# Turning the MLPs' inner activations and the output of seven heads by transposing transfers instead of on TensorE

## The chip, the cores and the metric

The kernel runs on one core of a Trainium2 chip. The metric is the device time of one execution in microseconds (us). The kernel before takes 2459.45 us, the median of three runs (2459.42, 2459.45 and 2463.46 us).

## The reference

A two-layer decoder trunk on one sequence of 256 tokens with 2048 channels, all in float32. Layer 0 is a retention layer with 8 heads, layer 1 a multi-head latent attention with 16 heads; each is followed by an MLP with 8192 inner channels. What matters here:

```python
def retention(...):
    ...
    o = o * lax.rsqrt(jnp.mean(o * o, axis=-1, keepdims=True) + RMS_EPS)   # per head, 512 values
    o = o.reshape(b, s, H * dv).astype(h.dtype)
    return (jax.nn.silu(gate) * o) @ w_out

def sq_relu_mlp(h, w1, w2):
    return jnp.square(jax.nn.relu(h @ w1)) @ w2
```

Both products need their left operand with the channel that is summed over on the partitions. The products that make that operand (`h @ w1`, a head's output) leave it with the tokens on the partitions. So between the two it has to be turned: 256 tokens x 8192 inner values in each MLP, 256 x 512 in each head.

## The kernel before, in words

**Products.** The 256 tokens are two tiles of 128 (t = 0, 1). Float32 accuracy comes from splitting each operand into a high and a low part (`split`, line 213): ScalarE rounds the high part (line 216), VectorE subtracts it to make the low part (line 217), and TensorE does three matmuls for one product (lines 409 to 411: high by high, high by low, low by high). Weights stream from HBM in quads of 1 MB (`quad`, line 321): one transfer issued by SP (SyncE) into one of three buffers `raw` (line 324), then split into tiles `wh` and `wl` (128 x 1024, five buffers each). A plain quad has eight products of 128x128 by 128x512. A quad "of seven" first forms sums of the weight blocks on VectorE (lines 363, 372 and 373), needs sums of the activations too (`with_sums`), and has seven products. `gemm_pair` (line 386) runs eight such quads and then takes the results out (`pair_out`, line 427): ScalarE copies six accumulators to SBUF (line 432), VectorE adds the rest (lines 434 to 448).

**The order of the work.** A program queue sets it: `tick` counts one per quad, `later(n, fn)` puts fn n ticks ahead, and at each tick the functions that are due write their instructions. Each engine runs its instructions in the order in which they end up in its list, and SP its transfers too.

**The MLPs.** `mlp` (line 864) has four groups in each layer. A group does two pairs of the first weight matrix (called here the even and the odd pair, 8 quads each; `u_` in the names), then two pairs of the second (`d_`). When a pair `u_` is done its result (2 token tiles x 2 blocks of 512 values) goes to `up` (line 871): four Relu on ScalarE (line 877), then `turn(0)` and, a tick later, `turn(1)`. A `turn` takes one block of 512 values of both token tiles and turns it in two halves k2. For each half, `transposed` (line 230) does four 128x128 transposes on TensorE into a PSUM bank (line 235), ScalarE squares the bank into SBUF (line 886), and the result is split (`hid`) and, for odd halves, summed (`hid_sum`, `hid_more`). A block thus has 8 transposes; a group has four blocks, two of the even pair and two of the odd one. The even pair's blocks are turned while the odd pair's quads run, the odd pair's while the first `d_` pair runs; that one needs the odd pair's blocks in its quads 4 to 7.

**The heads.** `ret_out` (line 748) makes a head's output y (two token tiles x 512), and its `turn` (line 767) turns it in the same way, 8 transposes a head, while the next head's quads run (for the last head, those of the output projection).

**Buffers.** The small SBUF tiles of 2 KB a partition all come from one ring of 14 (`f2k`, line 72).

Of the kernel before, what the change touches and what calls it, by code (L numbers as in the profile page):

```python
# [14 lines left out]
I32 = mybir.dt.int32  # L15
AF = mybir.ActivationFunctionType
# [19 lines left out]
P = 128  # L36
NT = 2
S = NT * P
# [28 lines left out]
def yoco(ctx: ExitStack, tc: tile.TileContext, a):  # L67
# [162 lines left out]
    def transposed(srcs, name):  # L230

        tp = bank("tp", [2, S], name)
        for j in range(2):
            for t in range(NT):
                nc.tensor.transpose(tp[:, j, t * P : (t + 1) * P], srcs(t, j), ident)
        return tp

# [510 lines left out]
    def ret_out(h, s, v, gate, y_act):  # L748
# [17 lines left out]

        def turn():
            for k2 in range(2):
                tp = transposed(lambda t, j: ys[t][:, (2 * k2 + j) * P : (2 * k2 + j + 1) * P], f"ytp{h}{k2}")
                yt = act_tile(f"y{h}{k2}")  # L770
                more = None
                if len(y_act) in (HEAD if h < RH // 2 else LATE):
                    u = f2k([2, S], f"yu{h}{k2}")
                    nc.scalar.copy(u, tp)
                    split_act(yt, u)
                    more = with_sums(u, f"y{h}{k2}")
                else:
                    split_act(yt, tp)
                y_act.append((yt, more))
# [84 lines left out]
    def mlp(layer, act, r, done):  # L864
        w1, w2 = a[f"mlp_w1_{layer}"], a[f"mlp_w2_{layer}"]
        f0 = 0
        for gi, nf in enumerate(GROUPS):
            hid, blocks = [], []
            last = gi == len(GROUPS) - 1

            def up(c, p, hid=hid, blocks=blocks):
# [3 lines left out]
                for t in range(NT):  # L875
                    for i in range(2):
                        nc.scalar.activation(c[t][i], c[t][i], AF.Relu, scale=r[t])

                def turn(i):
                    for q in (2 * i, 2 * i + 1):  # L880
                        name = f"hid{layer}_{p}{q}"
                        tp = transposed(
                            lambda t, j: c[t][q // 2][:, (q % 2 * 2 + j) * P : (q % 2 * 2 + j + 1) * P], f"{name}_tp"
                        )
                        u = f2k([2, S], f"{name}_u")
                        nc.scalar.activation(u, tp, AF.Square)
                        v = act_tile(name)
                        split_act(v, u)
                        blocks.append((v, with_sums(u, name) if len(blocks) in ODD else None))
                        hid.append(v)  # L890
# [402 lines left out]
```

## Time and profile before

| | |
|---|---|
| median of the runs | 2459.45 us |
| span of the profiled execution (first to last instruction) | 2456.3 us |
| TensorE matmul (PE) busy | 2446.2 us |
| VectorE (DVE) busy | 2212.2 us |
| ScalarE (ACT) busy | 1641.3 us |
| GpSimd (POOL) busy | 238.0 us |
| bytes moved by DMA | 521.05 MB, 212 GB/s |
| the two MLPs | 721 to 1389 us and 1774 to 2456 us of the span |

The profile lists instructions by engine, source line, operation and tile: `u_c<-u_wh,n` is a matmul that writes the accumulator `u_c` from the weights `u_wh` and the activations `n`. Start and duration are in microseconds, means in nanoseconds. PE is TensorE's matmuls, PEld its weight loads; matmuls overlap in the pipeline, so the time that one costs is the step from its start to the start of the next, not its duration. The profiled execution's own time is not listed apart from its span; the median of the runs lies 3.15 us above the span.

### The profile page before, as it was taken

What the parts mean: (1) busy time and instruction counts of PE and PEld (TensorE: products, weight loads), DVE (VectorE), ACT (ScalarE), POOL (GpSimd) and SP (SyncE); (2) the same over time, 40 slices, a digit from 0 to 9 for tenths busy, and PEclk for the clock granted to TensorE, in tenths of its full rate; (3) what the DMA queues carried; (4) which work ended last, traced back from release to release, by engine and by line L of the source; (5) the groups of instructions that cost most, each with busy time, mean ns of one, the idle gap of its engine ahead of it and who ended that gap; (6) DMA issues with size and microseconds to landing.
All of it is one profiled execution on the core that took longest, in us unless ns stands there. A gap on an engine that the chain in (4) does not pass through costs nothing.

```text
span 2456.3 us, 31721 instructions
## 1 busy us (share of the span) xinstructions
PE 2446.2 (100%) x11614; PEld 2057.6 (84%) x11614; DVE 2212.2 (90%) x2919; ACT 1641.3 (67%) x2307; POOL 238.0 (10%) x287
## 2 busy tenths in 40 slices
PE   9999999999999999999999999999999999999999
PEld 7888888888888888888888888998888888888887
DVE  7899899888899999999999998777899999999998
ACT  6566666556676767667676777577667667676674
POOL 6400001000000010010110001101000100100100
PEclk9999999999999999999999999999999999999999
DMA  8555569556565586695786555444555865957854
GB/s 309 207 201 191 192 202 259 191 183 224 197 218 194 196 254 218 207 272 187 241 253 213 200 202 180 155 162 173 197 199 205 252 228 194 262 198 229 264 209 170
DMA packets 93692, 521.05 MB, mean 212 GB/s; under 512 B 11104, under 2 KB 12512, under 8 KB 40288
## 3 DMA queue, kind: packets, MB, share of 16 engines
q1 hardware_dynamic: 72144, 472.83, 55.2%
q0 software_dynamic: 21248, 46.15, 8.9%
q8 instruction: 91, 1.49, 0.2%
q14 instruction: 65, 0.53, 0.1%
q10 hardware_dynamic: 144, 0.05, 0.0%
HBM read 479.14 MB, written 39.85 MB: 211 GB/s over the span
## 4 chain that ended last, share of the span: by engine, by line
PE 92%; DVE 2%; ACT 1%; issue 0%; DMA 0%; POOL 0%; ACTq 0%; DVEq 0%
PE u_c L411 7%; PE u_c L410 7%; PE u_c L409 7%; PE d_c L411 6%; PE d_c L410 6%; PE d_c L409 6%; PE rp_c L411 3%; PE rp_c L409 3%; PE rp_c L410 3%; PE u_p L411 2%; PE u_p L410 2%; PE u_p L409 2%; PE rq_acc L307 2%; PE rk_acc L307 2%; PE ro_c L411 2%; PE ro_c L409 2%
## 5 line engine op out<-in xcount | busy, mean ns | idle before, releaser
L217 DVE TENSOR_TENSOR d_wl<-d_raw,d_wh 128x1024 fp32r<-128x1024 f32 (+1 forms) x256 | 278.7, 1111 | 31.6 <-ACT d_wh L216 31.6
L217 DVE TENSOR_TENSOR u_wl<-u_raw,u_wh 128x1024 fp32r<-128x1024 f32 (+1 forms) x256 | 279.3, 1113 | 29.8 <-ACT u_wh L216 29.8
L409 PE MATMUL u_c<-u_wh,n 128*128 128x512 f32 x712 | 278.3, 392 | 0.0
L411 PE MATMUL u_c<-u_wh,n 128*128 128x512 f32 x712 | 277.2, 389 | 0.0
L410 PE MATMUL u_c<-u_wl,n 128*128 128x512 f32 x712 | 277.2, 389 | 0.0
L409 PE MATMUL d_c<-d_wh,hid 128*128 128x512 f32 x706 | 275.4, 392 | 0.5 <-ACT d_wh L216 0.5
L411 PE MATMUL d_c<-d_wh,hid 128*128 128x512 f32 x706 | 275.0, 390 | 0.0
L410 PE MATMUL d_c<-d_wl,hid 128*128 128x512 f32 x706 | 274.8, 389 | 0.0
L216 ACT CAST u_wh<-u_raw 128x1024 fp32r<-128x1024 f32 (+1 forms) x256 | 241.3, 973 | 49.6 <-PE u_c L411 24.1
L216 ACT CAST d_wh<-d_raw 128x1024 fp32r<-128x1024 f32 (+1 forms) x256 | 240.3, 971 | 39.9 <-PE d_c L411 16.6
L216 ACT CAST d_wh<-d_u 128x1024 fp32r<-128x1024 f32 x106 | 108.1, 1051 | 119.7 <-DVE d_u L373 82.6
L216 ACT CAST u_wh<-u_u 128x1024 fp32r<-128x1024 f32 x104 | 106.2, 1052 | 116.0 <-DVE u_u L373 77.3
L411 PEld LDWEIGHTS u_c<-u_wh,n 128*128 128x128 f32 x712 | 133.7, 188 | 27.8
L410 PEld LDWEIGHTS u_c<-u_wl,n 128*128 128x128 f32 x712 | 133.8, 188 | 27.4 <-DVE u_wl L217 0.3
L409 PEld LDWEIGHTS u_c<-u_wh,n 128*128 128x128 f32 x712 | 133.7, 188 | 27.0
L409 PEld LDWEIGHTS d_c<-d_wh,hid 128*128 128x128 f32 x706 | 132.6, 188 | 28.2 <-ACT d_wh L216 1.4
L411 PEld LDWEIGHTS d_c<-d_wh,hid 128*128 128x128 f32 x706 | 132.5, 188 | 27.6
L410 PEld LDWEIGHTS d_c<-d_wl,hid 128*128 128x128 f32 x706 | 132.6, 188 | 27.5 <-DVE d_wl L217 0.4
L216 ACT CAST rp_wh<-rp_raw 128x1024 fp32r<-128x1024 f32 x112 | 103.8, 945 | 74.2 <-PE rp_c L411 49.2
L217 DVE TENSOR_TENSOR rp_wl<-rp_raw,rp_wh 128x1024 fp32r<-128x1024 f32 x112 | 119.7, 1090 | 16.4 <-ACT rp_wh L216 16.2
L217 DVE TENSOR_TENSOR u_wl<-u_u,u_wh 128x1024 fp32r<-128x1024 f32 x104 | 123.5, 1222 | 3.1 <-ACT u_wh L216 2.8
L217 DVE TENSOR_TENSOR d_wl<-d_u,d_wh 128x1024 fp32r<-128x1024 f32 x106 | 125.8, 1221 | 0.0
(570 smaller groups left out, 6505.3 us busy)
## 6 DMA issues: line engine op xcount, KB each, us to landing
u_raw<-in_mlp_w SPq DMA_DIRECT2D x128, 1024.0 KB, 5.4
d_raw<-in_mlp_w SPq DMA_DIRECT2D x128, 1024.0 KB, 4.9
rp_raw<-in_ret_w_gv SPq DMA_DIRECT2D x56, 1024.0 KB, 4.8
ro_raw<-in_ret_w_out SPq DMA_DIRECT2D x32, 1024.0 KB, 4.9
uq_raw<-in_mla_w_uq SPq DMA_DIRECT2D x24, 768.0 KB, 4.3
rq_raw<-in_ret_w_qk SPq DMA_DIRECT2D x16, 1024.0 KB, 4.9
rk_raw<-in_ret_w_qk SPq DMA_DIRECT2D x16, 1024.0 KB, 4.8
xh<-d_c POOLq DMA_DIRECT2D x48, 256.0 KB, 6.1
```

Source lines behind the costliest of these rows:

```text
L216: nc.scalar.copy(h, src)
L217: return nc.vector.tensor_tensor(l, src, h.bitcast(F32), op=ALU.subtract)
L307: nc.tensor.matmul(acc[f], wh[:, cols], a.rearrange("p i s -> p (i s)"), start=k == 0, stop=k == nk - 1)
L409: nc.tensor.matmul(dst, ah, bh, start=n == 0, stop=False)
L410: nc.tensor.matmul(dst, ah, bl, start=False, stop=False)
L411: nc.tensor.matmul(dst, al, bh, start=False, stop=n == total[key] - 1)
```

## The change

Of the four blocks of a group in each MLP, three are no longer turned on TensorE: both blocks of the even pair and block 1 of the odd pair. Block 0 of the odd pair stays (`turn_on_pe`). Heads 0 to 6 are no longer turned on TensorE either; head 7 stays. That takes 8 transposes from each of 24 blocks and 7 heads.

In their place, a 32-bit value is seen as two 16-bit halves. `turn_by_dma` copies each token tile's 128x512 block on ScalarE into a tile with all low and all high halves apart (`parts`, 128 x 2 x 512 of 16 bits): two copies of 1024 elements a block. Two or three ticks later SP issues four transposing transfers of 128x512 16-bit values, SBUF to SBUF (two token tiles x two halves), into two tiles `turned`. Then, for each k2, `joined` puts the halves together again: two copies of 512 elements on ScalarE into `u`, which is squared in place (MLP) and split as before. The Relu of a block moves from `up` to its `turn`. The outputs of the heads now always go by way of a tile `u` in SBUF; before, some were split straight from PSUM.

```diff
+    def halves_of(v):
+        return v.bitcast(U16).rearrange("p (n two) -> p two n", two=2)
+
+    def turn_by_dma(blocks, name, wait, steps, then):
+
+        parts = [f2k([2, 512], f"{name}_h{t}", U16) for t in range(NT)]
+        for t in range(NT):
+            nc.scalar.copy(parts[t], halves_of(blocks[t]))
+
+        def turn():
+            turned = [f2k([4, S], f"{name}_t{i}", U16) for i in range(2)]
+            for t in range(NT):
+                for i in range(2):
+                    nc.sync.dma_start_transpose(turned[i][:, :, t * P : (t + 1) * P], parts[t][:, i])
+            for k2 in range(2):
+                later(steps[k2], lambda k2=k2: then(turned, k2))
+
+        later(wait, turn)
+
+    def joined(turned, k2, u):
+
+        for i in range(2):
+            dst = halves_of(u.rearrange("p j s -> p (j s)"))[:, i]
+            nc.scalar.copy(dst, turned[i][:, 2 * k2 : 2 * k2 + 2].rearrange("p j s -> p (j s)"))
...
         def turn():
+            if h < RH - 1:
+                turn_by_dma(ys, f"y{h}", 3, (0, 1), join)
+                return
             for k2 in range(2):
                 tp = transposed(lambda t, j: ys[t][:, (2 * k2 + j) * P : (2 * k2 + j + 1) * P], f"ytp{h}{k2}")
...
                 need(r, NT)
                 c = summed(c)
-                for t in range(NT):
-                    for i in range(2):
-                        nc.scalar.activation(c[t][i], c[t][i], AF.Relu, scale=r[t])
-
-                def turn(i):
-                    for q in (2 * i, 2 * i + 1):
...
+                def turn(i):
+                    for t in range(NT):
+                        nc.scalar.activation(c[t][i], c[t][i], AF.Relu, scale=r[t])
+                    if p % 2 and not i:
+                        turn_on_pe()
+                        return
+                    turn_by_dma(
+                        [c[t][i] for t in range(NT)], f"hid{layer}_{p}{i}", 2 if p % 2 else 3, (0, 1),
+                        lambda turned, k2: square(turned, i, k2),
+                    )
+
+                def square(turned, i, k2):
+                    name = f"hid{layer}_{p}{2 * i + k2}"
+                    u = f2k([2, S], f"{name}_u")
+                    joined(turned, k2, u)
+                    nc.scalar.activation(u, u, AF.Square)
+                    split_up(u, name)
```

49 lines of the change are left out of this document (27 added, 22 removed).

## The prediction

> **What bounds the kernel now.** I read the page first (engines, chain), then what TensorE waited for, then the places where it transposes, then each stretch of the MLPs.
>
> ```profile
> span 2456.3 us, 31721 instructions
> PE 2446.2 (100%) x11614; PEld 2057.6 (84%) x11614; DVE 2212.2 (90%) x2919; ACT 1641.3 (67%) x2307; POOL 238.0 (10%) x287
> PE 92%; DVE 2%; ACT 1%; issue 0%; DMA 0%; POOL 0%; ACTq 0%; DVEq 0%
> ```
>
> ```profile
> PE idle L131 <- DVE zeros L128: 1.2, 1, 1.2
> PE rg_acc L279 <- ACT a L218: 0.7, 1, 0.7
> ```
>
> The chain that ends last is 92% TensorE, and these two rows are TensorE's longest waits in the whole run, both in its first microseconds. So TensorE is not merely busy, it is fed: in the MLPs and heads what it no longer has to do comes off the time, as long as the others can feed it that much faster. DVE at 90% is the next limit.
>
> **What is removed.** A block's eight transposes, in the list of PE's matmuls and in the chain:
>
> ```profile
> 770.56 0.40 PE L411 MATMUL u_c<-u_wh,n 128*128 128x512 f32 x1
> 770.79 1.03 PE L235 MATMUL hid_tp<-cst,u_c 128*128 128x128 f32 x8
> 771.58 0.47 PE L409 MATMUL u_c<-u_wh,n 128*128 128x512 f32 x1
> 771.90 0.39 PE L410 MATMUL u_c<-u_wl,n 128*128 128x512 f32 x1
> 772.12 0.39 PE L411 MATMUL u_c<-u_wh,n 128*128 128x512 f32 x1
> 772.35 0.40 PE L409 MATMUL u_c<-u_wh,n 128*128 128x512 f32 x1
> ```
>
> ```profile
> 237.09 0.87 PE ytp L235 x8
> 770.95 0.87 PE hid_tp L235 x8
> ```
>
> From 771.90 to 772.35 are two plain steps, 0.45 us. The two steps from 770.56 to 771.90 take 1.34 with the transposes between them, so these cost 0.89; the chain has 0.87, for a head's block as for an MLP's. I take 0.88. Removed are 24 blocks (3 of 4, 4 groups, 2 layers) and 7 heads, 31 in all: 31 x 0.88 = 27.3 us, all on the path. That is the most that there is to gain.
>
> **What is added, engine by engine.** I look at one group, by pair: odd `u_` pair (the even pair's two blocks are turned in it), first `d_` pair (the odd pair's two blocks), then two pairs without any; last a head.
>
> ```profile
> 765.30:808.60 43.30, 43.30 (x200) 36.03 (x200) 40.96 (x52) 31.62 (x43) 0.00 (x0) 1.00 0.57 195
> 808.60:851.90 43.30, 43.30 (x200) 36.02 (x199) 41.39 (x52) 31.61 (x43) 0.00 (x0) 1.00 0.56 195
> 851.90:892.70 40.80, 40.80 (x181) 33.80 (x180) 37.49 (x41) 25.55 (x31) 6.96 (x8) 1.00 0.89 257
> 892.70:933.50 40.80, 40.80 (x181) 33.80 (x180) 37.06 (x41) 25.47 (x31) 6.90 (x8) 1.00 0.90 257
> 160.00:228.00 68.00, 68.00 (x336) 57.31 (x335) 62.59 (x96) 41.89 (x56) 2.44 (x6) 1.00 0.55 189
> ```
>
> (Columns: length, busy time of PE, PEld, DVE, ACT, POOL, then the clock and the DMA share.)
>
> ScalarE, per block: two copies of 1024 elements and four of 512. The trace has no copy of 16-bit halves; the nearest rows are 32-bit ones of the same counts.
>
> ```profile
> 767.13 2.97 ACT L216 CAST u_wh<-u_raw 128x1024 fp32r<-128x1024 f32 x3
> 769.97 2.22 ACT L877 ACTIVATE u_c<-u_c,n_r 128x512 f32<-128x512 f32 x3
> 806.93 1.08 ACT L432 COPY u_c<-u_c 128x512 f32<-128x512 f32 x2
> 807.88 1.10 ACT L432 COPY u_p<-u_p 128x512 f32<-128x512 f32 x2
> ```
>
> Three casts of 1024 take 2.84 us from start to start, 0.95 each; two copies of 512 take 0.95, 0.475 each. A block adds 2 x 0.95 + 4 x 0.475 = 3.8 us; squares and splits stay as many as they were. Over 31 blocks that is 118 us on an engine with 815 idle; it costs nothing as long as it is hidden. The cover is thinnest in the odd `u_` pair: two blocks bring ACT from 31.6 to 39.2, while PE falls from 43.3 to 41.5 there. In the first `d_` pair it is 35.4 of 42.4, in a head some 46 of 67. The copies' price from both sides: no saving from below the 32-bit price can shorten anything, since ACT is not the path; twice the price is the third rival.
>
> VectorE does the same work as before, only later. In the odd `u_` pair that is 40.96 us in 41.5. Its 2.3 idle us sit at the pair's end:
>
> ```profile
> 805.63 1.23 DVE L217 TENSOR_TENSOR d_wl<-d_raw,d_wh 128x1024 fp32r<-128x1024 f32 x1 [1.76 <-ACT d_wh L216]
> 785.03 1.23 DVE L217 TENSOR_TENSOR u_wl<-u_u,u_wh 128x1024 fp32r<-128x1024 f32 x1
> 786.87 0.19 PEld L410 LDWEIGHTS u_p<-u_wl,n_more 128*128 128x128 f32 x1
> ```
>
> The first row's wait can shrink without harm. The other two are the thinnest place of the pair: a `wl` ends at 786.26, TensorE loads it at 786.87, 0.6 us ahead. This is where the blocks' splits and sums crowd the start of the pair now; moved three ticks on, they leave that start and fall among quads 4 to 6, so the lead should first grow, then be used up. With DVE at 99% of the pair, a late ScalarE instruction can still make TensorE wait. I allow 0.5 us in each of the eight odd `u_` pairs, 4 us: between nothing and the 1.8 that the pair saves, nearer to nothing as the first `d_` pair, next, has 1.0 to spare and the two after it 3 each.
>
> SP, per block: four transposing transfers of 128 KB, each holding SP and its queue for some time w, and a wait of SP for the copies. Behind them stand the weight loads.
>
> ```profile
> u_raw<-in_mlp_w SPq DMA_DIRECT2D x128, 1024.0 KB, 5.4
> dec<-in_decay SPq DMA_DIRECT2D x8, 128.0 KB, 4.9
> 765.04 0.33 SPq L324 DMA_DIRECT2D u_raw<-in_mlp_w  x1
> 772.58 0.33 SPq L324 DMA_DIRECT2D u_raw<-in_mlp_w  x1
> 776.66 0.33 SPq L324 DMA_DIRECT2D u_raw<-in_mlp_w  x1
> 815.85 0.33 SPq L324 DMA_DIRECT2D d_raw<-in_mlp_w  x1
> L152 POOL DMA_DIRECT2D xh<-d_c x48 | 41.6, 866 | 784.6 <-DVE d_wl L217 439.6 <-ACT d_p L432 229.3 <-DVE u_wl L217 109.2
> q1 hardware_dynamic: 72144, 472.83, 55.2%
> ```
>
> No transposing transfer is in this trace. From below: SP's 0.33 us for an issue; the bytes themselves, at q1's rate (472.83 MB in 55.2% of 2456 us, 349 GB/s), are 0.38. From above: 4.9, the landing of a 128 KB transfer, if each waited for the one before. I take 0.9, near the 0.866 that GpSimd takes to issue one, as a transposing issue is the more laborious.
>
> Does 0.9 stay hidden? The even pair's first four transfers stand behind the load of 765.04 and ahead of that of 772.58 (quad 4). They wait for the copies: the Relus end near 770.7 once two are left for later, then 1.9 of copies, so 772.6. Quad 4's load goes at 772.6 + 4w and lands 5.4 later; the second block's transfers go ahead of quad 5's load, now at 776.66, which goes no earlier than 772.9 + 8w. Where they are needed:
>
> ```profile
> 783.66 1.06 ACT L216 CAST u_wh<-u_raw 128x1024 fp32r<-128x1024 f32 x1 [0.23 <-PE u_c L411]
> 788.23 0.39 PE L409 MATMUL u_c<-u_wh,n 128*128 128x512 f32 x1
> 788.44 1.23 DVE L363 TENSOR_TENSOR u_u<-u_raw 128x1024 f32<-128x1024 f32 x1
> 791.03 1.82 DVE L217 TENSOR_TENSOR u_wl<-u_raw,u_wh 128x1024 fp32r<-128x1024 f32 x2
> 793.67 0.39 PE L409 MATMUL u_p<-u_wh,n 128*128 128x512 f32 x1
> 826.95 1.05 ACT L216 CAST d_wh<-d_raw 128x1024 fp32r<-128x1024 f32 x1 [0.22 <-PE d_c L411]
> ```
>
> Quad 4 is first cast at 783.66, and cast plus subtraction leave 2.3 us to the matmul at 788.23; with everything 1.8 earlier the load must land by 784.2: w up to 1.5. Quad 5's sum starts at 788.44; what follows from it (the first `wl`, at 791.03 with 1.23) is 1.4 ahead of its matmul at 793.67, so with everything 1.8 earlier its load must land by 788.0: w up to 1.2. In the first `d_` pair the load of 815.85 goes behind one block's transfers, whose copies end near 818 (772.6 + 43.3, and 2 for block 0's squares), and is first cast at 826.95: w up to 1.3. At 0.9 all three hold, and the turned data (some 5 us after the issue) is there before ScalarE reaches the joining copies, two ticks or about 10 us after the first copies.
>
> [...]
>
> **The sum.** 2456.3 - 27.3 + 4 = 2433.0 us of span. The median lies 3.15 above the span of the profiled execution, so 2436.
>
> **The rivals.**
>
> First, the odd `u_` pairs are full: with 39.2 us of ACT and 40.96 of DVE in 41.5, one in-order engine waiting for the other costs all that the even blocks save there, 8 x 1.76 = 14.1, and perhaps the odd blocks' 8 x 0.88 = 7.0 too. For it: DVE's 0.6 us of lead. Against it: the lead grows where the splits leave. 2456.3 - 27.3 + 14.1 to 21.1, plus 3.15: 2446 to 2453, and a little more if the heads, at 62.59 of 67.1, lose some as well.
>
> Second, slower: the transposing transfers hold SP or its queue so long that weight loads come late. By the limits above, a group loses 8(w - 1.2) in the odd `u_` pair and 4(w - 1.3) in the `d_` pair, that is 12w - 14.8, against the 2.6 that it saves. A group gains nothing from w = 1.45 on, the whole, with the heads' 7 x 0.88 = 6.2, from 1.5. At 1.7 a group loses 3.0 net, eight groups 24, less the heads' saving: 2477. At 2 it is 2506, at 3 about 2602. For it: a wait in SP's order ahead of loads that now go out the moment a buffer is free, and an upper bound of 4.9. Against it: every issue that the trace has is under 0.9. [...]
>
> Third, also slower: ScalarE takes twice as long over 16-bit elements four bytes apart. Then the odd `u_` pair has 31.6 + 15.2 = 46.8 us of ACT in 41.5, 5.3 too many, eight times: 2433.0 - 4 + 42.4 + 3.15 = 2475. Nothing in the trace speaks for it but that no row excludes it.
>
> That the edit removes less than it says is a small one: the count of transposes shows it.
>
> **How the numbers follow.** A measurement of this kernel can tell about 0.2%, 5 us, from no change. The forecast (2431 to 2443) has a chance of 0.54. The first rival has 0.15, about half of it faster by more than 0.2% (below 2454.5) and half within it. The second has 0.25, the third 0.04, both slower. 0.02 are left for an edit that changes nothing. So faster is 0.62, within 0.2% is 0.09, slower is 0.29. The range starts at 2430, all of the 27.3 us gained and a little less time around the span, and reaches over the first rival into the second, to w of 1.7 and the third's price, 2478; some 0.18 of the second lies above it.
>
> **What would show it.** Right: 248 fewer transposes on line 235, no new wait of PE on `wl` or `wh`, the odd `u_` pair at about 41.5 to 42 us, ACT some 118 us busier, the transposing issues on SP under 1.2 us each. Wrong by the first rival: that pair stays near 43, with DVE waiting for ACT. By the second: ACT or DVE waiting for DMA on `u_raw` and `d_raw`, SP's loads late by several us behind the transposing issues, pairs longer than before. By the third: copies of 16-bit halves at about 1.9 us. The whole is wrong if the joining copies wait long for `turned`, which I take to be there in time.

## The result

The changed kernel takes 2479.95 us (median of four runs, 2479.22 to 2483.16), the kernel before, on the same chip, 2459.43 (2459.33 to 2463.46). The ratio is 1.0081, with a 95% interval of 1.0067 to 1.0096: slower by 0.8%. The forecast was 2436, in a range of 2430 to 2478. The span of the profiled execution is 2478.2 us against 2456.3. One execution of e17_plain5_x_on_sp below took 3435.88 us at a granted clock of 0.665, and its ratio there leaves it out.

### The profile page after: what moved, and what is told of

It reads as the page before. It is cut to its first block, busy times and chain, and to the rows that moved or that the text cites. A ratio compares the mean times of both kernels' runs of the same rounds, so it can differ in the third digit from the quotient of the medians.

```text
span 2478.2 us, 31655 instructions
## 1 busy us (share of the span) xinstructions
PE 2439.2 (98%) x11366; PEld 2025.8 (82%) x11366; DVE 2217.0 (89%) x2919; ACT 1756.3 (71%) x2489; POOL 241.9 (10%) x287
## 2 busy tenths in 40 slices
DMA packets 161150, 537.32 MB, mean 217 GB/s; under 512 B 78560, under 2 KB 79968, under 8 KB 107744
## 4 chain that ended last, share of the span: by engine, by line
PE 59%; DVE 13%; ACT 12%; issue 6%; DMA 4%; POOL 1%; SPq 1%; ACTq 0%; DVEq 0%; POOLq 0%
PE d_c L436 4%; PE d_c L437 4%; PE d_c L435 4%; PE u_c L436 3%; PE u_c L437 3%; PE u_c L435 3%; DVE u_wl L218 2%; DVE rp_wl L218 2%; ACT u_wh L217 2%; ACT d_wh L217 2%; PE rq_acc L333 2%; PE rp_c L435 2%; PE rp_c L436 2%; PE rp_c L437 2%; DMA hid_t<-hid_h 2%
## 5 line engine op out<-in xcount | busy, mean ns | idle before, releaser
L217 ACT CAST d_wh<-d_raw 128x1024 fp32r<-128x1024 f32 (+1 forms) x256 | 239.4, 972 | 27.7 <-ACT d_wh L217 12.1
L436 PEld LDWEIGHTS d_c<-d_wl,hid 128*128 128x128 f32 x706 | 132.5, 188 | 38.0 <-DVE d_wl L218 10.4
```

The costliest lines, as they stand in the source:

```text
L217: nc.scalar.copy(h, src)
L436: nc.tensor.matmul(dst, ah, bl, start=False, stop=False)
```

## The profile after

(The edit moves the lines: 409 to 411 are now 435 to 437, 216 and 217 are 217 and 218, 363, 372 and 373 are 389, 398 and 399, 432 is 458.) The page, engines and chain:

```profile
span 2478.2 us, 31655 instructions
PE 2439.2 (98%) x11366; PEld 2025.8 (82%) x11366; DVE 2217.0 (89%) x2919; ACT 1756.3 (71%) x2489; POOL 241.9 (10%) x287
PE 59%; DVE 13%; ACT 12%; issue 6%; DMA 4%; POOL 1%; SPq 1%; ACTq 0%; DVEq 0%; POOLq 0%
```

248 transposes are gone (11614 to 11366 instructions) and ScalarE has 115 us more, where 118 was forecast. But the chain that ends last is TensorE's for 59% only, where it was 92%: it now runs through VectorE, ScalarE and transfers. PE's busy time fell by 7.0 us and not by 27.3: part of what TensorE loses lies inside its busy time (below, 42.47 us busy in a pair for which it needs 41.5), and the rows of its waits show only the rest. What TensorE waited for:

```profile
PE u_c L436 <- DVE u_wl L218: 8.6, 10, 1.1
PE d_p L436 <- DVE d_wl L218: 6.4, 8, 0.8
PE u_p L436 <- DVE u_wl L218: 3.7, 11, 0.6
PE rp_c L435 <- DVE rk_u L730: 2.0, 4, 0.8
```

These are new: TensorE stands at low parts that VectorE hands over late. By stretches of the same group and one period of the heads (columns as in the prediction: length, PE, PEld, DVE, ACT, POOL, clock, DMA share):

```profile
770.80:814.70 43.90, 42.47 (x184) 34.09 (x183) 40.29 (x51) 38.78 (x54) 0.00 (x0) 1.00 0.77 213
814.70:859.00 44.30, 43.40 (x193) 34.82 (x191) 42.68 (x53) 35.92 (x50) 0.00 (x0) 1.00 0.61 204
859.00:899.80 40.80, 40.80 (x182) 33.78 (x180) 37.50 (x41) 25.54 (x31) 6.96 (x8) 1.00 0.90 258
171.90:240.50 68.60, 67.44 (x327) 56.17 (x327) 62.46 (x82) 44.90 (x61) 2.90 (x4) 1.00 0.66 206
```

The odd `u_` pair, 43.30 before, takes 43.90 although TensorE has 1.76 us less to do; the first `d_` pair went from 43.30 to 44.30 although it has 0.88 less. The pairs without transposes are unchanged at 40.80. VectorE does the same work in the odd pair (40.29 us; 40.96 before) but stands idle for 3.6 us of it.

Measured from the first matmul of a pair to the first of the next, over all eight groups:

| | TensorE's own need | before | after | lost against the need |
|---|---|---|---|---|
| odd `u_` pair | 43.28 - 1.76 = 41.52 | 43.28 | 43.35 to 46.85, in sum 352.8 | 20.6 us |
| first `d_` pair | 43.28 - 0.88 = 42.40 | 43.28 | 44.29 to 44.90, in sum 355.5 | 16.3 us |
| heads (start of the MLP) | 721.3 - 6.2 = 715.1 | 721.3 | 726.8 | 11.7 us |

The three add up to 48.6 us; the span is 21.9 longer with 27.3 less to do, 49.2. So three places are to be explained.

SP's queue in an odd `u_` pair that begins at 940.6 (start, length of a run of equal issues):

```profile
948.32 5.20 SPq L252 DMA_TRANSPOSE hid_t<-hid_h  x4
953.62 0.52 SPq L350 DMA_DIRECT2D u_raw<-in_mlp_w  x1
954.24 5.53 SPq L252 DMA_TRANSPOSE hid_t<-hid_h  x4
```

A transposing issue holds SP for 1.3 us (5.20 / 4). The load between the fours is that of quad 5. Over all odd `u_` and first `d_` pairs, ScalarE and VectorE together wait 0.2 us for weight loads. ScalarE's new copies:

```profile
L262 ACT COPY hid_u<-hid_t 128x512 uint16<-128x512 uint16 x96 | 70.6, 769 | 36.9 <-DMA hid_t<-hid_h 36.8
L246 ACT COPY hid_h<-u_c 128x1024 uint16<-128x1024 uint16 x48 | 49.4, 1072 | 0.0
```

The joining copies wait 36.8 us in all for turned halves: 14.1 in the odd `u_` pairs, 22.8 in the first `d_` pairs. In the odd pair from 940.6 on, ScalarE's list and then VectorE's:

```profile
954.84 0.78 ACT L262 COPY hid_u<-hid_t 128x512 uint16<-128x512 uint16 x1 [1.05 <-DMA hid_t<-hid_h]
955.49 1.04 ACT L217 CAST u_wh<-u_u 128x1024 fp32r<-128x1024 f32 x1
956.43 0.78 ACT L262 COPY hid_u<-hid_t 128x512 uint16<-128x512 uint16 x1
957.25 0.63 ACT L933 ACTIVATE hid_u<-hid_u 128x512 f32<-128x512 f32 x1
```

```profile
956.56 1.22 DVE L218 TENSOR_TENSOR u_wl<-u_u,u_wh 128x1024 fp32r<-128x1024 f32 x1 [1.04 <-ACT u_wh L217]
959.04 0.69 DVE L218 TENSOR_TENSOR hid<-hid_u,hid 128x512 fp32r<-128x512 f32 x1 [1.26 <-ACT hid L217]
```

A joining copy and its wait stand ahead of a weight cast, and two more copies and the square ahead of the cast of the block; VectorE waits for both casts, 2.3 of the 3.2 us that it idles in this pair. From there to the pair's end it has next to no idle time (21.50 us busy of the last 22.00), and TensorE stands 0.87 us for a low part at 970.45.

The first `d_` pair from 984.0 on, ScalarE's list and then VectorE's:

```profile
993.32 2.01 ACT L246 COPY hid_h<-u_c 128x1024 uint16<-128x1024 uint16 x2
996.68 0.65 ACT L217 CAST hid_more<-hid_sum 128x512 fp32r<-128x512 f32 x1
1000.33 1.65 ACT L262 COPY hid_u<-hid_t 128x512 uint16<-128x512 uint16 x2 [3.01 <-DMA hid_t<-hid_h]
1001.85 1.99 ACT L217 CAST d_wh<-d_u 128x1024 fp32r<-128x1024 f32 x2
```

```profile
998.81 0.69 DVE L399 TENSOR_TENSOR d_u<-d_u,d_raw 128x512 f32<-128x512 f32 x1
999.42 1.82 DVE L218 TENSOR_TENSOR d_wl<-d_raw,d_wh 128x1024 fp32r<-128x1024 f32 x2
1002.92 2.36 DVE L218 TENSOR_TENSOR d_wl<-d_u,d_wh 128x1024 fp32r<-128x1024 f32 x2 [1.68 <-ACT d_wh L217]
```

The sum `d_u` is ready at 999.5. ScalarE could cast it, but it stands for 3.01 us at the joining copies, which come first in its list; VectorE then waits 1.68 us for the cast.

## The experiments

Three theories at the start, **A** to **C**, and a fourth after the first four runs: **A**, ScalarE has too many copies; **B** (SP theory), the transposing issues hold SP and the weight loads come late; **C** (landing theory), ScalarE stands at its joining copies until the halves have landed, with weight casts behind; **D** (VectorE theory), VectorE has no time left in these pairs: what it idles there it cannot make up. All ratios are to the kernel before, measured again beside each run, with 95% intervals.

### One suspect at a time: e1_transfers, e2_copies

e1 is the kernel before with the 124 transposing transfers at their places on SP, of data that nobody uses (the low and high halves are not separated). e2 is the kernel before with the 16-bit copies on ScalarE, whose result is not used, and no transfers.

```diff
 # e1: before, beside the turns on TensorE
+    nc.sync.dma_start_transpose(turned[i][:, :, t * P : (t + 1) * P], src)
 # e2: before, beside the turns on TensorE
+    nc.scalar.copy(parts[t], halves_of(blocks[t]))
+    nc.scalar.copy(halves_of(u)[:, i], parts[k2][:, i])
```

> The kernel before, TensorE's transposes and all, with the 124 transposing transfers of SP beside it at the same places of SP's order; nothing reads what they write. Relative to before (2459.4), the change lost 47.8 us somewhere (27.3 hoped for, 20.5 slower). Theory A (copies): ScalarE's extra copies, in order ahead of the weight casts, starve VectorE and TensorE; then this kernel is at 2460, give or take 3. Theory B (transfers): SP and its queue are held, weight loads come late; then most of the 47.8 is here, 2490 to 2507. Theory C (wait): ScalarE stands at the joining copies until the turned data has landed; then 2460 as in A, for nothing waits for the data here.

> The kernel before, with the change's copies of 16-bit halves on ScalarE beside it (two of 1024 elements and four of 512 for each of the 31 blocks, at the same ticks), no transfers; nothing reads the last copies. Theory A: most of the 47.8 us is here, 2490 to 2507. Theories B and C: 2460, give or take 3, as ScalarE still has 28% idle time.

Measured: e1 2459.28 us, 0.9998 (0.9988 to 1.0007); e2 2462.23, 1.001 (1.000 to 1.002). All odd `u_` and first `d_` pairs stay at 43.28 in both. Alone, the transfers cost nothing that can be told, the copies some 2 us (at most 5 by the interval). But both still have TensorE's transposes as cover; they show that the loss needs the parts together or the cover gone.

### The joining copies later: e3_join_later

```diff
-                turn_by_dma(ys, f"y{h}", 3, (0, 1), join)
+                turn_by_dma(ys, f"y{h}", 3, (1, 2), join)
-                        [c[t][i] for t in range(NT)], f"hid{layer}_{p}{i}", 2 if p % 2 else 3, (0, 1),
+                        [c[t][i] for t in range(NT)], f"hid{layer}_{p}{i}", 2 if p % 2 else 3, (1, 2),
```

> The changed kernel with each joining copy one tick (one quad, about 5 us) later, copies and transfers as they are. Theory C: the 36.8 us of ScalarE waiting for the turned halves go, and the time falls by 20 to 45, to 2435 to 2460. Theories A and B: 2480, give or take 5, as the work on ScalarE and SP is the same.

Measured: 2509.70 us, 1.0203 (1.0188 to 1.0219): 30 us worse, which no theory had forecast. The odd `u_` pairs rise to 46.9 to 51.4 us, while the first `d_` pairs fall to 42.9 to 43.5, one to 44.6. ScalarE's wait for landings hardly changes (35.6 us). TensorE now waits 31.3 us for `u_wl` ahead of matmuls into `u_p` (3.7 in after), which only quads of seven have; that the splits and sums of the blocks come too late in VectorE's list is a reading, which no run tested.

### The copies on GpSimd: e4_gpsimd

```diff
-            nc.scalar.copy(parts[t], halves_of(blocks[t]))
+            nc.gpsimd.tensor_copy(parts[t], halves_of(blocks[t]))
-            nc.scalar.copy(dst, turned[i][:, 2 * k2 : 2 * k2 + 2].rearrange("p j s -> p (j s)"))
+            nc.gpsimd.tensor_copy(dst, turned[i][:, 2 * k2 : 2 * k2 + 2].rearrange("p j s -> p (j s)"))
```

> The changed kernel with all copies of 16-bit halves on GpSimd, which is idle in the pairs that turn blocks. ScalarE then has less to do than before. Theory A, and C if the wait mattered only for what stands behind it on ScalarE: 2433 to 2445, if GpSimd's copies of 512 elements take about 1 us. Theory B: 2480, give or take 5.

Measured: 2577.15 us, 1.0476 (1.0460 to 1.0492). The groups of its page say why:

```profile
L246 POOL COPY hid_h<-u_c 128x1024 uint16<-128x1024 uint16 x48 | 126.2, 2653 | 356.9 <-ACT u_c L920 329.7 <-issue 27.2
L262 POOL COPY hid_u<-hid_t 128x512 uint16<-128x512 uint16 x96 | 118.9, 1303 | 47.7 <-DMA hid_t<-hid_h 40.0 <-issue 7.7
```

GpSimd takes 2.65 us where ScalarE takes 1.07. It tells nothing about A that the longer path would not hide.

### The heads as before: e5_heads_on_pe

The changed kernel, with heads 0 to 6 turned on TensorE as before.

```diff
-            if h < RH - 1:
-                turn_by_dma(ys, f"y{h}", 3, (0, 1), join)
-                return
...
```

> The changed kernel with the heads turned on TensorE as before; only the MLPs' blocks go by transfers. In the changed kernel's profile the first MLP starts 5.5 us later than before, where the seven heads should have saved 6.2. If the heads lose by themselves: 2474 to 2475, 5.5 less than the changed kernel. If what they lose shows only because of something else (loads, buffers): no change, 2480.

Measured: 2475.25 us, 1.0064 (1.0049 to 1.0079), 4.7 less than the changed kernel. The heads' part of the change loses by itself. The two largest of the heads' new waits in after are `rp_c <- DVE rk_u` (2.0 us) and `rp_c <- ACT rp_wh` (2.4), both gone in e5. The first fits this: in before a head's transposes (236.93 to 237.72) stand just ahead of these matmuls, VectorE reads the keys out of their accumulators from 237.99 on (`rk_u`, line 704 there), and the matmul at 238.50 does not wait; in after that reading begins at 241.88 (line 730), 1.41 us behind the first of these matmuls and not 0.27, and TensorE stands 0.36 us for it. The second lies in the first head's stretch, where weight casts come late. The two make 4.4 of the 11.7 us that the heads lost; the rest is not traced to a cause.

### Where the sevens stand: e6_sevens_early, e7_fewer_sevens

e6 moves the quads of seven of the odd `u_` and first `d_` pairs forward; e7 makes the one at place 5 plain, which gives VectorE less and TensorE 0.68 us more to do in each pair.

```diff
 # e6: the kinds, in an order (0, 2, 1, 3, 4, 5, 6, 7); the same in the first d_ pair
-                seven = SEVEN if p % 2 else ODD if p else LATE
+                seven = (1, 3, 7) if p % 2 else ODD if p else LATE
 # e7, and the same in the kinds of the first d_ pair
-                seven = SEVEN if p % 2 else ODD if p else LATE
+                seven = (3, 7) if p % 2 else ODD if p else LATE
```

> The changed kernel with the quads of seven of the odd first-layer pair and of the first second-layer pair at places 2, 3 and 7 of the pair and not 3, 5 and 7 (the same number of them, the same work). Theory D: VectorE needs nearly the whole of these pairs, idles 2 to 3 us in their middle, when it has caught up and ScalarE's list holds the joining copies, and lacks that time when the turned blocks' splits and the quads of seven come together at places 4 to 7; then it now has work ahead of the middle and plain quads where the blocks arrive, and the pairs come near 41.8 and 42.7 us in place of 43.7 and 44.4: 2445 to 2455. Theory C, the wait of ScalarE for the turned halves alone: it stays as long, 2480 give or take 4. Theory A, the number of ScalarE's copies: 2480 give or take 4.

> The changed kernel with the quads of seven at place 5 of the same pairs made plain: in each of 16 pairs VectorE has 4.1 us less to do and TensorE 0.68 us more. Theory D, VectorE's time is what is short: the pairs come near their TensorE time, 42.2 and 43.1, 2453 to 2462. If VectorE's time isn't short (theories A and C): 16 times 0.68 more, 2491.

Measured: e6 2503.41 us, 1.0187 (1.0170 to 1.0204), a miss: with the same work the sevens come before ScalarE and VectorE can serve them (TensorE waits 21.0 us for `u_wh`, 16.0 for `d_wl`). e7 2469.12, 1.0039 (1.0024 to 1.0054): 11 us faster although TensorE has 16 x 0.68 = 10.9 us more to do. An odd `u_` pair and the first `d_` pair of e7:

```profile
938.90:981.10 42.20, 42.20 (x187) 34.92 (x187) 37.25 (x47) 38.22 (x53) 0.00 (x0) 1.00 0.75 225
981.10:1025.30 44.20, 43.44 (x195) 35.63 (x194) 37.49 (x47) 33.80 (x47) 0.00 (x0) 1.00 0.63 202
```

With 37.25 us of VectorE, 3.0 less than in after, the odd pair takes what TensorE needs (41.52 + 0.68 = 42.2), with ScalarE as full as in after; so do six of the eight, the two others take 43.2 and 43.9. ScalarE still waits 12.1 us for landings in these pairs (14.1 in after), and VectorE idles even longer, but has room for it. So in the odd pairs D holds, with one limit: the edit also takes out that quad's chain of sum, cast and subtraction, and no run parts the chain from VectorE's time. The first `d_` pairs do not improve (44.3 to 45.0), though VectorE has 5.2 us less in the one shown: they lose to something else.

### No wait for the landing: e8_no_wait

The joining copies read the halves that ScalarE has separated, so that the blocks are not turned; the transfers still run, for nobody.

```diff
-                later(steps[k2], lambda k2=k2: then(turned, k2))
+                later(steps[k2], lambda k2=k2: then(parts, k2))
-            nc.scalar.copy(dst, turned[i][:, 2 * k2 : 2 * k2 + 2].rearrange("p j s -> p (j s)"))
+            nc.scalar.copy(dst, turned[k2][:, i])
```

> The changed kernel with the joining copies reading the copied halves instead of the turned ones: transfers and copies all run as before, but nobody waits for a transfer to land, and the blocks aren't turned. Theory C: the 37.8 us that ScalarE stands at the joining copies go, and most of what was lost with them: 2435 to 2450. Theory D: only the part of VectorE's idle time in mid-pair that comes from that wait goes, about 1 us of 2.6 in the odd first-layer pair and most of 1.7 in the other: 2455 to 2470. Theory A: 2480 give or take 4.

Measured: 2488.01 us, 1.0115 (1.0100 to 1.0130). The first `d_` pairs fall to 42.9, two of them to 43.4 and 43.6, near their need of 42.40, as C has it. The odd `u_` pairs rise to 45.8 to 49.6. VectorE's waits and SP's queue in one that begins at 938.6:

```profile
DVE u_u L389 <- DMA u_raw<-in_mlp_w: 47.3, 15, 7.4
```

```profile
946.25 10.83 SPq L252 DMA_TRANSPOSE hid_t<-hid_h  x8
957.19 8.01 SPq L350 DMA_DIRECT2D u_raw<-in_mlp_w  x3
```

The edit changed SP's order: all eight transposing issues, 1.35 us each, stand ahead of the load of quad 5, which in after stands between the two fours. Counted from the start of the pair that load goes 5.6 us later than in after (18.6 against 13.0), and VectorE waits for it. B's mechanism exists, but it is not what after suffers from (there `u_u` waits 4.7 us in all, before it was 6.1, and none of it in the odd pairs).

### VectorE relieved by GpSimd: e9_low_parts_pool

```diff
+    def split_act_pool(v, src):
+        nc.scalar.copy(v[:, :, 0], src)
+        nc.gpsimd.tensor_tensor(v[:, :, 1], src, v[:, :, 0].bitcast(F32), op=ALU.subtract)
...
-                    split_act(v, u)
+                    split_act_pool(v, u)
```

> The changed kernel, in which GpSimd instead of VectorE subtracts the low part of each quarter of the inner activations (64 subtractions of 0.685 us, four of them in each odd u_ pair and four in each first d_ pair; 0.60 us apart when they stand back to back, so 2.4 us of VectorE a pair). TensorE, ScalarE, SyncE and all transfers have the same work. If VectorE's time is what is short in these pairs (VectorE theory), the odd u_ pair falls from 43.4 to 43.9 to about 42 (TensorE alone 41.5) and the first d_ pair from 44.4 to about 43.2 (TensorE alone 42.4): 8 x 1.6 and 8 x 1.2, so 2457 us, 2450 to 2464. If it is ScalarE that stands at the joining copies until the turned halves have landed and holds the weight casts behind them (landing theory), that wait is the same and the time stays at 2474 to 2480. If SyncE's queue is held too long (SP theory), 2480.

Measured: 2498.32 us, 1.0158 (1.0141 to 1.0175), above every forecast. The time line shows why, with GpSimd's subtraction beside VectorE's:

```profile
970.72 1.21 DVE L218 TENSOR_TENSOR u_wl<-u_u,u_wh 128x1024 fp32r<-128x1024 f32 x1
971.24 1.85 POOL L233 TENSOR_TENSOR hid<-hid_u,hid 128x512 fp32r<-128x512 f32 x1 [3.73 <-ACT hid L232]
972.09 2.08 DVE L218 TENSOR_TENSOR u_wl<-u_u,u_wh 128x1024 fp32r<-128x1024 f32 x1 [0.15 <-ACT u_wh L217]
974.09 1.21 DVE L218 TENSOR_TENSOR u_wl<-u_raw,u_wh 128x1024 fp32r<-128x1024 f32 x1
```

VectorE's subtraction of 1.21 us takes 2.08 while GpSimd works (so in all eight odd pairs; 2.31 in the first `d_` pairs), so the 0.6 us that each moved subtraction saves VectorE comes back as a longer neighbour. VectorE is busy for 41.4 us of the odd pair from 942.0 on, with four instructions less than in after, where it was 40.2. And GpSimd's own subtractions, 1.28 us at the least, take up to 5.3, so the low parts also come later. The experiment does not speak against D: VectorE was not relieved.

### Each pair for itself: e10_d_later, e11_even_only, e12_odd_only

```diff
 # e10: the joining copies a quad later in the first d_ pair alone
-                        [c[t][i] for t in range(NT)], f"hid{layer}_{p}{i}", 2 if p % 2 else 3, (0, 1),
+                        [c[t][i] for t in range(NT)], f"hid{layer}_{p}{i}", 2 if p % 2 else 3, (1, 2) if p % 2 else (0, 1),
 # e11: only the even pair's blocks by transfers
-                    if p % 2 and not i:
-                        turn_on_pe()
+                    if p % 2:
+                        turn_on_pe(i)
 # e12: only the odd pair's block 1 by transfers
+                    if not (p % 2 and i):
+                        turn_on_pe(i)
```

> The changed kernel with only one thing moved: in the first d_ pair the joining copies of the odd u_ pair's second block are queued one weight tile later; the odd u_ pairs keep theirs. Landing theory: ScalarE no longer stands 3 us in front of the turned halves there, the first d_ pair falls from 44.4 to about 43 us (the run without the wait had 42.9), 8 x 1.4 = 11 us, so 2469 us, 2465 to 2473. VectorE theory: the subtraction and the sums of this block come later still and fall among the seven-product tiles, so the pair stays at 44.4 or gets longer: 2479 to 2490. SP theory: no change, 2480.

> The changed kernel, in which only the two blocks of every even u_ pair go by transfers and both blocks of the odd u_ pair are turned on TensorE: the first d_ pair gets 8 x 0.11 = 0.88 us of TensorE back and loses its transfers and joining copies. If each pair's loss is its own, the odd u_ pair stays at 43.4 to 43.9 and the first d_ pair is back at 43.3 as before: 8 x 1.1 = 9 us less, 2471 us, 2467 to 2474. If the first d_ pair's loss is a debt that the odd u_ pair before it leaves on VectorE, it stays at 44.4 or is 45.2: 2480 to 2487.

> The changed kernel, in which only the second block of every odd u_ pair goes by transfers and the three other blocks of a group are turned on TensorE: the odd u_ pair is as in the kernel before, 43.3. If each pair's loss is its own, the first d_ pair stays at 44.4: with the 5 us that the heads lose 2459.4 + 8 x 1.1 + 5 = 2473 us, 2469 to 2477. If it is a debt from the odd u_ pair, the first d_ pair falls to 42.5 to 43: 2459.4 - 8 x 0.5 + 5 = 2460 us, 2457 to 2464.

Measured: e10 2481.98 us, 1.0089 (1.0074 to 1.0104); e11 2475.14, 1.0060 (1.0045 to 1.0075); e12 2481.29, 1.0085 (1.0070 to 1.0100). In e12 the odd `u_` pairs are back at exactly 43.28 and the first `d_` pairs lose still more (45.1 to 45.8); in e11 the first `d_` pairs are at 43.6 and the odd pairs at 43.3 to 43.9, one at 48.5. So neither loss is the other's debt. e12 lies above both its forecasts: its first `d_` pairs lose more than in after, and ScalarE waits longer for landings there (31.3 us, in after 22.8); why it does is not shown.

In e10 the first `d_` pairs fall to 43.3 to 43.8, near the number that C forecast, but not by C's way: ScalarE's wait for landings is 40.8 us in all, not less. What the edit moved in effect is the second quarter of the block: the first joining copies, which wait for the landing, begin 16.5 us into the pair (16.4 in after). What TensorE waited for in the first `d_` pair of the second group, in after, in e10 and in e8:

```profile
PE d_p L436 <- DVE d_wl L218: 0.8, 1, 0.8
PE d_c L436 <- DVE d_wl L218: 0.5, 1, 0.5
```

```profile
PE d_c L436 <- DVE d_wl L218: 0.5, 1, 0.5
```

```profile
PE d_p L436 <- DVE d_wl L218: 0.6, 1, 0.6
```

After has two stalls: one at `d_c` behind ScalarE's stand for the landing, which goes when nothing is waited for (e8), and one at `d_p`, where the second quarter's work on VectorE comes before weights that are due, which goes when that work comes later (e10). In the usual pair of 44.3 us, e8 takes away 1.4 us and e10 1.0, with what follows each stall. The gain of e10 is given back in the second `d_` pairs (41.3 instead of 40.8) and in one odd pair (47.1), so its total is what D forecast.

### VectorE or the rest, and the parts put together: e13_even_plain5, e16_all_plain5

e13 is e11 with the heads on TensorE and the quad at place 5 of the odd `u_` pairs plain. e16 has the three blocks by transfers, the heads on TensorE, that quad plain, and e10's edit.

```diff
-                seven = SEVEN if p % 2 else ODD if p else LATE
+                seven = (3, 7) if p % 2 else ODD if p else LATE
```

> The changed kernel with three parts of it taken back or altered: the heads' output and both blocks of the odd u_ pair are turned on TensorE as before, so that only the two blocks of each even u_ pair go by transfers, and the weight tile at place 5 of the odd u_ pairs takes eight products a step instead of seven (0.68 us more of TensorE, about 4.1 us less of VectorE a pair; the first d_ pairs keep their sevens). If the odd u_ pair's loss is VectorE's missing time, it takes what TensorE alone needs, 42.2 us against 43.28 before, and the first d_ pair is 43.3 as before: 2459.4 - 8 x 1.1 = 2450.5 us, 2449 to 2454, faster than both kernels. If the landing of the turned halves or SyncE's held queue is what costs there, the sevens don't matter, the pair stays at 43.6 and gets the 0.68 on top: 8 x 1.0 more than before, 2465 to 2468.

> The changed kernel with the heads on TensorE as before, the joining copies of the first d_ pair a weight tile later, and eight products a step at place 5 of the odd u_ pairs; all three blocks of a group still go by transfers. VectorE theory for the odd u_ pairs and landing theory for the first d_ pairs together: 42.2 and 43.3 us where before had 43.28 and 43.28, and 0.5 us more in each second d_ pair: 2459.4 - 8 x 1.1 + 8 x 0.5 = 2454.6 us, 2451 to 2459. If either is wrong, 2463 to 2470.

Measured: e13 2468.72 us, 1.0034 (1.0021 to 1.0046), above its forecast; e16 2462.47, 1.0012 (1.0004 to 1.0021). In e16 the odd pairs are 42.2 to 42.6, as D has it; the first `d_` pairs have 43.2 to 44.8 and the second ones 41.3. In e13 six of the odd pairs are 42.2 to 43.8 and the first `d_` pairs 43.28, but the odd pair of the last group of each MLP takes 48.3 and 47.4 us. The waits of ScalarE and the transfers there (1269.9 on):

```profile
ACT hid_u L262 <- DMA hid_t<-hid_h: 7.7, 1, 7.7
```

```profile
q0 software_dynamic: 607, 1.95, 24.4%
u_raw<-in_mlp_w SPq DMA_DIRECT2D x5, 1024.0 KB, 7.4
x_mlp<-xh POOLq DMA_DIRECT2D x4, 256.0 KB, 5.4
hid_t<-hid_h SPq DMA_TRANSPOSE x8, 8.5
```

In the last group GpSimd's queue q0 reads the residual stream (`x_mlp`) at that time. The transposing transfers land 8.5 us after their issue there (median), not 4.1 as over all 96 of after, and ScalarE stands 7.7 us. e16 has the same reads, but GpSimd issues the last at 1275.1, ahead of the first transposing transfer at 1280.2, and its pair takes 42.6; in e13 two are issued as late as 1281.3 and 1281.8, amid the issues of the transposing transfers (1277.6 to 1294.8).

### The length of ScalarE's burst: e14_square_later

```diff
                     joined(turned, k2, u)
-                    nc.scalar.activation(u, u, AF.Square)
-                    split_up(u, name)
+                    def finish():
+                        nc.scalar.activation(u, u, AF.Square)
+                        split_up(u, name)
+                    later(0.5, finish)
```

> The changed kernel, in which the squaring and the split of a joined quarter are queued half a weight tile after its joining copies, so that ScalarE's burst ahead of the weight casts is 1.3 us and not 2.5. If VectorE's idle time in mid pair comes from the length of that burst, the odd u_ pair falls to 42.0 to 43.0 and the time to 2468 to 2476. If VectorE's whole time is what counts, whatever order ScalarE has, its subtractions and sums come half a tile later and fall among the later tiles: odd u_ pair 44 to 46, 2484 to 2500. If only the landing counts, it is 2478 to 2482.

Measured: 2481.72 us, 1.0089 (1.0074 to 1.0105). The total is that of the landing theory, but the pairs aren't: four odd pairs are at 43.2 to 43.8 as in after, four at 45.2 to 48.3, the first `d_` pairs at 43.1, the second at 41.3. It is inconclusive between the theories; a shorter burst alone does not help.

### The transfers earlier: e15_transfers_earlier

```diff
-                        [c[t][i] for t in range(NT)], f"hid{layer}_{p}{i}", 2 if p % 2 else 3, (0, 1),
+                        [c[t][i] for t in range(NT)], f"hid{layer}_{p}{i}", 1 if p % 2 else 2, (1, 2),
```

> The changed kernel with the transfers of the inner activations queued one weight tile earlier and their joining copies where they were. On SyncE's queue all eight transfers of the even u_ pair's two blocks then stand ahead of the sixth load of the odd u_ pair, instead of four ahead of it and four behind. Landing theory: no wait of ScalarE for turned halves is left, the first d_ pair falls to 43 us and the odd u_ pair to 42 to 43: 2459 to 2469 us. SP theory: eight issues of 1.3 us in a row make that sixth load about 5 us late, VectorE and ScalarE wait for it as in the run in which the copies didn't wait, the odd u_ pair is 45 to 48 and the first d_ pair 43: 2484 to 2500 us.

Measured: 2507.20 us, 1.0189 (1.0175 to 1.0203), more than either forecast. The odd pairs have 46.0 to 50.8 with `u_u` waiting 21.6 us for `u_raw`: with eight issues ahead of quad 5's load B decides, as in e8. The first `d_` pairs stay at 44.3 to 44.9, because nothing moved there: the transfers wait for ScalarE's 16-bit copies (SP stands 21.1 us for them in after, 8 times), so the first issue is 10.5 us into the pair shown where it was 10.4 in after, and ScalarE's wait for the landing (38.6 us in all) is much the same.

### The reads beside the transfers: e17_plain5_x_on_sp, e18_x_on_sp

e17 is e13, e18 the changed kernel, each with one thing more: SP issues the reads of the residual stream, behind the last odd `u_` pair's transfers.

```diff
-                nc.gpsimd.dma_start(x[t][b], x_home[t][b])
+                nc.sync.dma_start(x[t][b], x_home[t][b])
```

> The kernel of e13 with one thing more: the eight 256 KB reads of the residual stream that end each MLP are issued by SyncE and not by GpSimd; in SyncE's order they stand behind the transfers of the last odd u_ pair, so that they no longer run beside them. In e13 these two odd u_ pairs took 48.3 and 47.4 us, with one wait of 7.7 us of ScalarE for turned halves, while the same pairs of the other groups took 42.2 to 43.8. If the wait is long because those reads share the DMA engines with the transposing transfers, both pairs fall to 42.2 to 43 and the time by 10 to 11 us, from 2468.7 to 2458, 2455 to 2461: level with the kernel before or a little faster. If something else makes them long (VectorE's work of the last group, or SyncE's order), they stay at 47 to 48: 2466 to 2470.

> The changed kernel with nothing else than those reads of the residual stream on SyncE instead of GpSimd. There one of the two last odd u_ pairs is long (46.85 us, the other 43.65). If the reads beside the transfers make it long, it falls to 43.5 and the time to 2475 to 2478; the second is not helped. If not, 2480 stays.

Measured: e17 2455.13 us, 0.9979 (0.9969 to 0.9988), faster than both kernels; the gain lies in the odd pairs, 341.0 us over the eight against 346.2 before. e18 2483.42, 1.0094 (1.0081 to 1.0108), a miss. The odd pair of the last group in e17:

```profile
1268.90:1311.10 42.20, 42.20 (x187) 34.92 (x187) 37.34 (x47) 38.21 (x53) 0.00 (x0) 1.00 0.80 232
```

Both last pairs fall from 48.3 and 47.4 to 42.16 (in the first of them ScalarE's wait is 1.0 us instead of 7.7 and the median landing 5.3 instead of 8.5), while three others still take 42.9 to 44.0: reads beside the transposing transfers made them land late. In e18 the long odd pair falls from 46.85 to 44.91 only, and the first `d_` pairs of the last groups rise to 46.8 and 46.1: there the reads, now in SP's queue, stand among the transposing transfers of the odd pair's block 1, which e17 does not have.

## Why the prediction was wrong, point by point

**What is removed: right in kind.** The 248 transposes are gone, and where the others can feed TensorE their time is gained: in e17 an odd pair with 0.68 us more of matmuls takes 42.16 at best, 1.12 less than before, and the MLP pairs without transposes are unchanged. It is a ceiling that the changed kernel does not reach in any of the three places.

**ScalarE's copies: nearly right, and not the cost.** The joining copies take 0.63 us from start to start and not 0.475, so a block has 4.4 us and not 3.8; ScalarE gained 115 us (118 forecast) and has 38.8 in the odd pair (39.2). At 4.4 us the 31 blocks would make 136, so that the total still came near 118 is partly luck. Alone the copies cost some 2 us (e2). The third rival, twice the price, did not happen.

**The step that failed: "VectorE does the same work as before, only later", with 0.5 us for each odd pair, 4 us in all.** The work is the same, but VectorE also needs its inputs in time. It had 40.3 us to do in 41.5 and idles 3.6 us of the pair, because ScalarE's list puts joining copies, squares and casts of the blocks, and a wait for the landing, ahead of the casts that VectorE needs next (over the eight pairs VectorE waits 15.9 us for weight casts and 10.2 for casts of the blocks). Before, its 2.3 idle us were free, since TensorE needed 43.3 anyway. So the odd pairs lost 20.6 us, not 4. e7 and e16 show it from the other side: with 3 us less of VectorE's work the pair takes TensorE's time or up to 0.5 us more (in e7 two of the eight take 1.0 and 1.8 more), with the joining copies and their waits still in ScalarE's list. The first rival had this very mechanism, at 0.15, and capped its price at what the odd pairs save; they ended longer than before, which its working did not allow.

**"The first `d_` pair, next, has 1.0 to spare": wrong.** It lost 16.3 us over eight groups. VectorE's 41.4 of 42.4 us is no spare time when ScalarE stands 3 us in front of data that have not landed. The prediction named that wait as what would make the whole wrong, and took the data to be there, as it put the joining copies about 10 us behind the first 16-bit copies. In the pair shown ScalarE is at them 4.0 us after it began those (993.32 to 997.33), while the transfers wait for the 16-bit copies and the fourth lands 6.7 us after the first issue; and the joining copies of the first quarter stand ahead of casts that are already possible. e8 and e10 show two stalls, worth some 1.4 and 1.0 us a pair, one by this wait and one by the second quarter's work on VectorE.

**The heads: wrong, at nothing.** They lost 11.7 us against the forecast, and undoing their part gave 4.7 back (e5); the transposes covered a wait of TensorE behind the next head's keys. That they were cover is read from the waits, and accounts for part of the loss; no run filled that place with other work.

**The second rival (SP): the price was mis-sized, the mechanism is real but not the cause.** A transposing issue holds SP for 1.3 us, not 0.9, above the limit of 1.2 that the prediction had worked out for quad 5. The prediction had eight issues ahead of quad 5's load. In after four stand ahead of it and four behind, so that limit does not apply, and the transfers alone cost nothing (e1). Even by the rival's own formula 1.3 us would take only 0.8 of the 2.6 that a group saves. That the measured time lies near the 2477 of w = 1.7, and near the third rival's 2475, is chance. Where the eight do stand ahead (e8, e15), the odd pair takes 45.8 to 50.8. It is the issue that is long, not the landing: a plain load of 1 MB holds SP for 0.33 us in the profile of before, while the landing took 4.1 us in the median, against 4.9 for a plain load of 128 KB before. Nor is every issue of before under 0.9: the longest on SP (line 242) and on GpSimd (line 152) take 0.96.

What stays open: how much of the odd pairs' idle time is the landing and how much ScalarE's order. In the pair shown ScalarE waits 1.05 us for the landing and VectorE idles 3.2. No run took one away and left the other (e8 and e15 changed SP's order, e14 shifted VectorE's work).

## What to carry to other kernels

When work is taken off the busiest engine, the next engine's share of the new, shorter time is the wrong measure; look at its idle time inside the stretch and ask what its inputs wait for, because idle time that was free becomes the bound (here VectorE's 2.3 us of an odd pair). A wait for a transfer in the middle of an engine's list costs what stands behind it (here ScalarE stood 3.01 us for a landing, and VectorE 1.68 for the cast behind it), so the landing has to be ahead of the list, not on average but in the stretch where other transfers run beside it (a median of 8.5 us there, 4.1 over all). And a change that loses as a whole can win in part: here two of four blocks, with 3 us of VectorE's work in that stretch given up for 0.68 of TensorE's, and the reads beside the transfers moved.

## What the runs showed of the hardware

- A transposing SBUF-to-SBUF transfer of 128x512 16-bit values holds SP for 1.3 us (1.19 to 3.15) and lands 4.1 us after its issue (2.5 to 9.1; medians of the 96 of the MLPs in after); in the last group's odd pair of the first MLP the median landing is 8.5 us beside reads of another queue (e13), 5.3 without them (e17). With the 124 transfers the kernel has 78560 packets under 512 bytes (after), without them 11104 (before).
- Beside a subtraction on GpSimd of 128x512 (1.28 us at least, 1.80 in the median), VectorE's subtraction of 128x1024, 1.21 us alone, takes up to 2.08 in the odd pairs and 2.31 in the first `d_` pairs (e9). What slows it is not shown.
- GpSimd's copy of 16-bit halves takes, in the MLPs, 2.65 us for 128x1024 (1.07 on ScalarE) and 1.30 for 128x512 (0.77); in the heads 1.24 for 128x1024 (1.05) and 1.37 for 128x512 (0.77) (e4 and after).
